# Loads in another order: a smaller first slice, the rotation table last, residual tiles in later steps

## The chip, the cores and the metric

The kernel runs on one core of a Trainium2 chip. A core has a matrix engine (TensorE, PE in the profile; its weight loads are PEld), a vector engine (VectorE, DVE), an engine for functions of one variable (ScalarE, ACT), a general one (GpSimd, POOL) and SyncE (SP), which here only issues transfers (DMAs). Each engine has its own queue of instructions, and semaphores tie the queues together. Sixteen DMA engines carry out the transfers of all queues. The metric is the device time of one execution in microseconds, the median of several.

## The reference

One layer of a streaming encoder, on x of 1024 frames by 1024 channels, all in 32-bit floats:

```
h = rms_norm(x, g_mix);  z = h @ w_in          # queries, keys, values, indexer, gates, ...
y_a = chunked attention with relative bias     # 4 heads, 9 chunks of 64 frames
y_b = attention on the 256 keys that an indexer picks for each frame
      # index score = sum over 4 heads of relu(q_i . k_i) * w_i, q_i and k_i rotated (rope)
y_c = gated linear recurrence over time
merged = sum over the three branches of sigmoid(gate) * (y @ w_branch)
x = x + merged @ w_out
gu = rms_norm(x, g_ffn) @ w_ffn_in;  x = x + (silu(gu[:, :2816]) * gu[:, 2816:]) @ w_ffn_out
```

What matters here are the two ends: the norm of x with the product that gives the indexer's 324 columns (256 query, 64 key, 4 weights), and the last product, with the residual x added to it.

## The kernel before

**Precision.** Every large product runs on operands that are split in two: `hi`, the value rounded to the matrix engine's format (an ACT copy, line 101), and `lo`, what is left (a DVE subtraction, line 102). `mm3` (lines 116 to 119) then issues three matmuls: hi by hi (L117), hi by the right side's lo (L118), lo of the left side by hi (L119). In the profile nearly all matmuls therefore stand on these three lines, and nearly all splits on lines 101 and 102; the names of the tiles tell them apart.

**Buffers.** `Slots` keeps a list of equal buffers in SBUF: `get` takes the one that was freed first, `free` puts one back at the end. A tile in a buffer that was used before waits until the last use of the old one is over. `sl` is the large pool, `ring` a small one (seven buffers at the start, 31 in the last product).

**Order.** A planner of the tile framework arranges the instructions of each engine by its own estimate of when their inputs are ready; the order of the program is kept only where `keep_in_program_order` says so, as for the loads that this case is about. [...]

**The start.** x is read twice: as rows (for the norm's sum of squares, on ACT, line 187) and transposed (as the left side of products). The eight tiles of 128 frames come in batches of 1, 1, 2, 2 and 2 (`BATCH`). The SyncE queue gets the rows and transposes of batch 0, the small constants `sm`, the index weights in slices of k (`W0K`; k runs over eight blocks of 128 channels, 324 columns each), batch 1, batch 2, the rotation table `ctab` (512 KB), batches 3 and 4. For each batch GpSimd computes the reciprocal root, PE spreads it over partitions (L190), DVE scales the transposed tile (L197), ACT and DVE split it (hTh, hTl). `split_w0`, called in the k loop of batch 0, splits a slice of weights (w0h, w0l). PE then runs 24 matmuls of 324 columns for each tile of 128 frames (G<-w0h,hTh and so on). The rotation table is first used by DVE on lines 279 and 280, when four tiles are through.

**The last product.** Activations come from HBM, where the feed-forward step has left them (`pair_dram`, tile fa<-pd), the weights from `w_fo` (fw). It is a Strassen-like scheme: four passes m = 0 to 3 of eleven steps kk each, 44 steps; a step of passes 0 to 2 has 24 matmuls of 512 columns. `prep1` to `prep4` load and split the operands of a step, and `prepare` calls them four steps ahead (`AHEAD`). The eight tiles of the residual x (`load_x`, tile xr<-x2d, 512 KB each) are loaded in pass 0, one in each of `prep1(3)` to `prep1(10)`, behind the loads of that step. Tiles 0 to 3 are first added to (L1329) at the end of pass 0, tiles 4 to 7 (L1346) at the end of pass 1. All these loads share SyncE's queue; GpSimd's queue writes the last results of the feed-forward step at the same time.

Of the kernel before, what the change touches and what calls it, by code (L numbers as in the profile page):

```python
# [10 lines left out]
F32 = mybir.dt.float32  # L11
# [68 lines left out]
def hybrid_kernel(ctx: ExitStack, tc: tile.TileContext, x, xt, small, cs, bias_a, lru_w, w_idx, w_zg, w_c, w_g, w_b,  # L80
                  w_o, w_fi, w_fo, out):
    nc = tc.nc
# [5 lines left out]
    ring = Slots(arena, range(NRING))  # L88
# [7 lines left out]
    def smc(name, j=0, n=1):  # L96
        o, _ = SMALL_OFF[name]
        return sm[:, o + j:o + j + n]

    def split(raw, hi, lo, eng=None):  # L100
        S.activation(hi, raw, AF.Copy)  # L101
        (eng or V).tensor_tensor(lo, raw, hi.bitcast(F32), op=OP.subtract)  # L102
# [21 lines left out]
    def rsqrt(dst, src, n, scale):  # L124
        v = const.tile([128, n], F32, name="rs_v", tag=f"rsv{n}", bufs=2)
        G.tensor_scalar(v, src, scale, EPS, op0=OP.mult, op1=OP.add)
        G.tensor_tensor(dst, v, mhalf[:, 0:n], op=OP.pow)
# [7 lines left out]
    def sbank(shape=(128, 1024)):  # L135
        return psum.tile(list(shape), F32, name="S", tag="S", bufs=2)
# [6 lines left out]
    hT = [(sl.get((128, T), F32R, "hTh"), sl.get((128, T), F32R, "hTl")) for _ in range(KD)]  # L143

    w0 = []
    W0K = ((0, 3), (3, 3), (6, 2))

    def load_w0():
        for k0, kn in W0K:
            raw = ring.get((128, kn, 324), F32, "w0r")  # L150
            tc.keep_in_program_order(nc.sync.dma_start(raw, w_idx[:, k0:k0 + kn, :]))
            w0.append([k0, kn, raw])

    def split_w0(q):
        k0, kn, raw = w0[q]
        hi, lo = ring.get((128, kn, 324), F32R, "w0h"), ring.get((128, kn, 324), F32R, "w0l")
        split(raw, hi, lo)
        ring.free(raw)
        w0[q] = (k0, kn, hi, lo)
# [4 lines left out]
    for t0, tn in BATCH:  # L164
        for t in range(t0, t0 + tn):
            xts[t] = sl.get((128, D), F32, "x")
            tc.keep_in_program_order(nc.sync.dma_start(xts[t], x[t * 128:(t + 1) * 128, :]))
        kn = KD // tn
        ps_ = []
        for n in range(tn):  # L170
            c0 = 1024 * (t0 + n)
            pt = sl.get((128, kn, 128 * tn), F32, "xT")
            tc.keep_in_program_order(nc.sync.dma_start(pt.rearrange("p k t -> p (k t)"), xt[:, c0:c0 + 1024]))
            ps_.append(pt)
        parts.append(ps_)
        if t0 == 0:
            tc.keep_in_program_order(nc.sync.dma_start(sm, small))
            load_w0()
        if t0 == 2:
            ctab = sl.get((128, NT, 2, 64), F32, "cs")  # L180
            tc.keep_in_program_order(nc.sync.dma_start(ctab, cs))
    junk = sl.get((128, D), F32, "junk")
    for (t0, tn), ps_ in zip(BATCH, parts):
        w = 128 * tn
        rb = sbank((128, w))
        for t in range(t0, t0 + tn):
            S.activation(junk, xts[t], AF.Square, accum_out=ss_x[:, t:t + 1])
        rsqrt(rs_x[:, t0:t0 + tn], ss_x[:, t0:t0 + tn], tn, 1.0 / D)
        for t in range(t0, t0 + tn):
            PE.transpose(rb[:, 128 * (t - t0):128 * (t - t0) + 128], rs_x[:, t:t + 1].to_broadcast([128, 128]), ident)  # L190
        kn = KD // tn
        for k in range(KD):
            if t0 == 0 and k in (0, 3, 6):
                split_w0(k // 3)
            r = ps_[k // kn][:, k % kn]
            hi, lo = (a[:, 128 * t0:128 * t0 + w] for a in hT[k])
            V.scalar_tensor_tensor(r, r, smc("g_mix", k), rb, op0=OP.mult, op1=OP.mult)  # L197
            split(r, hi, lo)
        sl.free(*xts[t0:t0 + tn], *ps_)
# [1032 lines left out]
    ring = Slots(arena, fore + rw.free_list + rr.free_list + sl.free_list[:9])  # L1232
# [4 lines left out]
    def load(t, src):  # L1237
        tc.keep_in_program_order(nc.sync.dma_start(t, src))
        return t

    def split_pair(raw, n=2):
        if n == 1:
            t = ring.get((128, 2, 512), F32R, "fo")
            split(raw, t[:, 0:1], t[:, 1:2])
            return t[:, 0:1], t[:, 1:2], t
        hi, lo = ring.get((128, 2, 512), F32R, "foh"), ring.get((128, 2, 512), F32R, "fol")
        split(raw, hi, lo)
        return hi, lo, hi, lo
# [3 lines left out]
    def load_x(t):  # L1252
        xr.append(load(sl.get((128, D), F32, "xr"), x2_dram[t]))

    def split_act(m, kk):
        raw = load(ring.get((128, 2, 512), F32, "fa"), pair_dram[m][kk])
        a = split_pair(raw)
        ring.free(raw)
        return a

    def weights(kk, q):
        return load(ring.get((128, 2, 512), F32, "fw"), w_fo[kk, :, q:q + 2])

    def prep1(kk):
        B = weights(kk, 0)
        a = split_act(0, kk)
        if kk > 2:
            load_x(kk - 3)
        w = split_pair(B)
        ring.free(B)  # L1270
        return a, w

    def prep2(kk):
        B = ring.get((128, 512), F32, "fw")
        load(B, w_fo[kk, :, 1])
        b34[kk] = load(sl.get((128, 2, 512), F32, "fw2"), w_fo[kk, :, 2:4])
        a = split_act(1, kk)
        ts = ring.get((128, 2, 512), F32, "T12")
        V.tensor_sub(ts[:, 0], b34[kk][:, 0], B)
        V.tensor_sub(ts[:, 1], b34[kk][:, 1], ts[:, 0])  # L1280
        w = split_pair(ts)
        ring.free(ts, B)
        return a, w
# [12 lines left out]
    def prep4(kk):  # L1296
# [12 lines left out]

    plan = [  # L1310
        (prep1, ((0, 0, 1), (1, 1, 0))),
        (prep2, ((0, 1, 1), (1, 0, 0))),
        (prep3, ((0, 0, 0), (1, 1, 1))),
        (prep4, ((1, 0, 0),)),
# [158 lines left out]
```

## Time and profile before

| | |
|---|---|
| median of 3 runs | 1534.41 us (1532.22 to 1535.24) |
| the profiled execution | 1535.26 us, its span 1533.5 us |
| mean granted TensorE clock | 0.989 of full |
| PE, PEld busy | 1475.8 us (96%), 1233.4 us (80%) |
| DVE, ACT, POOL busy | 1127.5 us (74%), 760.6 us (50%), 110.6 us (7%) |
| DMA | 182.59 MB, 119 GB/s over the span |

An engine's busy time is the time in which at least one of its instructions ran, so PE can be busy and still wait a little between matmuls; "idle before" is the stretch in which an engine ran nothing, and the arrow behind it names what ended it. The last product runs from about 1320 us to the end. A fence below holds whole lines of a view; "..." stands for lines left out.

### The profile page before, as it was taken

The numbers are of one execution on the slowest core, as the hardware profiler recorded it, in microseconds if no ns is written. First come the engines' busy times: TensorE is split into PE (matmuls) and PEld (weight loads), VectorE is DVE, ScalarE is ACT, GpSimd is POOL, SyncE is SP. The second block draws the span as 40 slices with busy tenths as digits, with TensorE's granted clock in tenths as the row PEclk, the third lists the DMA queues.
The fourth block names the chain that finished last, engine by engine and source line by source line (L and its number), as shares of the span: only waits on it lengthen the run. The fifth ranks groups of instructions, "written<-read, shape, count | busy, mean of one in ns | idle before, by whom it ended". The sixth has DMA issues, their size and how long they took to land.

```text
span 1533.5 us, 19936 instructions
## 1 busy us (share of the span) xinstructions
PE 1475.8 (96%) x7556; PEld 1233.4 (80%) x7556; DVE 1127.5 (74%) x1997; ACT 760.6 (50%) x1204; POOL 110.6 (7%) x161
## 2 busy tenths in 40 slices
PE   6999899999999998999998989999999999999999
PEld 5898688989788976788886868888888888788887
DVE  6889989869666779767889786555555556478973
ACT  6557767865778656443114563333333333354440
POOL 1220011210000200110000200000000000000000
PEclk9999999999999999999999999999999999999999
DMA  7011213112111131358551322323232323697532
GB/s 285 28 46 54 85 32 110 31 68 84 55 54 43 44 106 44 133 170 319 188 196 66 115 91 97 110 96 110 96 110 97 110 96 124 247 349 267 191 125 89
DMA packets 52240, 182.59 MB, mean 119 GB/s; under 512 B 6000, under 2 KB 6128, under 8 KB 52144
## 3 DMA queue, kind: packets, MB, share of 16 engines
q1 hardware_dynamic: 38448, 135.17, 25.6%
q0 software_dynamic: 11968, 43.00, 7.2%
q10 hardware_dynamic: 1728, 3.15, 0.5%
q8 instruction: 59, 0.97, 0.3%
q14 instruction: 37, 0.30, 0.1%
HBM read 135.94 MB, written 45.35 MB: 118 GB/s over the span
## 4 chain that ended last, share of the span: by engine, by line
PE 63%; DVE 6%; issue 2%; ACT 2%; DMA 2%; POOL 0%; SPq 0%; ACTq 0%; POOLq 0%; DVEq 0%
PE B L118 14%; PE B L119 14%; PE B L117 14%; PE G L119 3%; PE G L117 3%; PE G L118 3%; PE T L118 1%; PE T L119 1%; PE T L117 1%; DMA fa<-pd 1%; PE S L117 1%; PE S L118 1%; PE S L119 1%; PE T L426 1%; PE T L418 1%
## 5 line engine op out<-in xcount | busy, mean ns | idle before, releaser
L118 PE MATMUL B<-hl,fwh 128*128 128x512 f32 x528 | 205.4, 391 | 2.8 <-DVE hl L102 2.8
L117 PE MATMUL B<-hh,fwh 128*128 128x512 f32 x528 | 202.7, 391 | 3.3 <-ACT hh L101 3.3
L119 PE MATMUL B<-hh,fwl 128*128 128x512 f32 x528 | 198.4, 391 | 0.0
L117 PEld LDWEIGHTS B<-hh,fwh 128*128 128x128 f32 x528 | 99.5, 188 | 25.0 <-ACT hh L101 4.2
L118 PEld LDWEIGHTS B<-hl,fwh 128*128 128x128 f32 x528 | 99.7, 189 | 24.4 <-DVE hl L102 3.9
L119 PEld LDWEIGHTS B<-hh,fwl 128*128 128x128 f32 x528 | 99.6, 189 | 20.7
L118 PE MATMUL G<-wzl,hTh 128*128 128x256 f32 x384 | 112.1, 293 | 3.5 <-DVE wzl L102 3.5
L117 PE MATMUL G<-wzh,hTh 128*128 128x256 f32 x384 | 110.9, 291 | 3.8 <-ACT wzh L101 3.1
L119 PE MATMUL G<-wzh,hTl 128*128 128x256 f32 x384 | 111.9, 292 | 0.0
L102 DVE TENSOR_TENSOR fwl<-s,fwh 128x1024 fp32r<-128x1024 f32 x44 | 53.9, 1224 | 77.9 <-PE B L118 75.1
L117 PE MATMUL B<-foh,foh 128*128 128x512 f32 x264 | 102.9, 396 | 2.1 <-ACT foh L101 2.1
L118 PE MATMUL B<-fol,foh 128*128 128x512 f32 x264 | 102.7, 389 | 0.0
L119 PE MATMUL B<-foh,fol 128*128 128x512 f32 x264 | 101.7, 389 | 0.0
L655 ACT ACTIVATE junk_s<-score,ngS 128x1024 int8<-128x1024 f32 (+2 forms) x78 | 77.5, 993 | 17.8 <-DVE ngS L653 13.7
L117 PEld LDWEIGHTS G<-wzh,hTh 128*128 128x128 f32 x384 | 75.3, 197 | 5.8 <-ACT wzh L101 3.7
L118 PEld LDWEIGHTS G<-wzl,hTh 128*128 128x128 f32 x384 | 75.4, 196 | 5.1 <-DVE wzl L102 4.1
L119 PE MATMUL G<-hTh,wgl 128*128 128x512 f32 x192 | 75.8, 395 | 2.0 <-DVE wgl L102 2.0
L117 PE MATMUL G<-hTh,wgh 128*128 128x512 f32 x192 | 75.8, 395 | 1.1 <-ACT ge L550 1.1
L119 PEld LDWEIGHTS G<-wzh,hTl 128*128 128x128 f32 x384 | 75.6, 197 | 0.7 <-issue 0.5
L118 PE MATMUL G<-hTl,wgh 128*128 128x512 f32 x192 | 75.5, 393 | 0.0
L101 ACT ACTIVATE fw<-fb 128x512 fp32r<-128x512 f32 x22 | 13.9, 634 | 121.4 <-PE B L119 120.5
L101 ACT ACTIVATE foh<-fa 128x1024 fp32r<-128x1024 f32 x33 | 35.0, 1060 | 58.7 <-DMA fa<-pd 39.5
(486 smaller groups left out, 3859.0 us busy)
## 6 DMA issues: line engine op xcount, KB each, us to landing
fw<-in_w_fo SPq DMA_DIRECT2D x33, 512.0 KB, 5.6
fa<-pd SPq DMA_DIRECT2D x33, 512.0 KB, 5.0
gl<-gd SPq DMA_DIRECT2D x24, 512.0 KB, 5.3
fa<-in_w_fi SPq DMA_DIRECT2D x22, 512.0 KB, 3.5
fb<-in_w_fi SPq DMA_DIRECT2D x22, 512.0 KB, 3.5
pd<-act POOLq DMA_DIRECT2D x22, 512.0 KB, 5.2
ga<-in_w_g SPq DMA_DIRECT2D x18, 512.0 KB, 3.6
x<-in_x SPq DMA_DIRECT2D x16, 512.0 KB, 7.2
```

Of the source, the lines that this page charges most:

```text
L101: S.activation(hi, raw, AF.Copy)
L102: (eng or V).tensor_tensor(lo, raw, hi.bitcast(F32), op=OP.subtract)
L117: PE.matmul(o, lhsT=lh, rhs=rh, start=first, stop=False, **kw)
L118: PE.matmul(o, lhsT=lh, rhs=rl, start=False, stop=False, **kw)
L119: PE.matmul(o, lhsT=ll, rhs=rh, start=False, stop=last, **kw)
L418: PE.transpose(pt[:, b - c0], P[:, 128 * b:128 * b + 128], ident)
L426: PE.matmul(o[64 * e:64 * e + 64, :], lhsT=v[(b0 + b) // 4][:, (b0 + b) % 4, h, :], rhs=PT[e][:, b, :], start=b == 0, stop=b == nb - 1, sk ...
L655: S.activation(junk_s[:, 0:(i + 1) * 128], score[i], AF.Sign, bias=self.ng.bitcast(F32)[:, j:j + 1], accum_out=self.cnt[:, j:j + 1])
```

## The change

Three edits, all to the order or the size of loads:

- The index weights come in slices of 2, 3 and 3 blocks of k, not 3, 3 and 2. The splits follow (k = 0, 2, 5, not 0, 3, 6).
- The rotation table is loaded behind the last batch of x, not behind the third.
- The residual tiles 0 to 3 are loaded in `prep1(6)` to `prep1(9)`, and tiles 4 to 7 in `prep2(1)` to `prep2(4)`, in the second pass.

```diff
-    W0K = ((0, 3), (3, 3), (6, 2))
+    W0K = ((0, 2), (2, 3), (5, 3))
...
-            load_w0()
-        if t0 == 2:
+            for q in range(len(W0K)):
+                load_w0(*W0K[q])
+        if t0 == 6:
             ctab = sl.get((128, NT, 2, 64), F32, "cs")
...
-            if t0 == 0 and k in (0, 3, 6):
-                split_w0(k // 3)
+            if t0 == 0 and k in (0, 2, 5):
+                split_w0((k + 1) // 3)
...
     def prep1(kk):
         B = weights(kk, 0)
         a = split_act(0, kk)
-        if kk > 2:
-            load_x(kk - 3)
+        if 6 <= kk < 10:
+            load_x(kk - 6)
...
     def prep2(kk):
...
         a = split_act(1, kk)
+        if 0 < kk < 5:
+            load_x(kk + 3)
```

`load_w0` now loads one slice of given place and size, and is called once for each.

## Rows read from the trace of the kernel before

**Rows 1.** The page's part 1: busy us, share of the span, instructions of each engine.

```profile
PE 1475.8 (96%) x7556; PEld 1233.4 (80%) x7556; DVE 1127.5 (74%) x1997; ACT 760.6 (50%) x1204; POOL 110.6 (7%) x161
```

**Rows 2.** Timeline of PE, 1337.6 to 1344: start, us, line, operation [idle before].

```profile
1337.78 0.39 PE L119 MATMUL B<-foh,fol 128*128 128x512 f32 x1
1340.28 3.60 PE L117 MATMUL B<-foh,foh 128*128 128x512 f32 x8 [2.11 <-ACT foh L101]
1343.72 0.39 PE L118 MATMUL B<-fol,foh 128*128 128x512 f32 x1
```

**Rows 3.** Windows: length, busy of PE, PEld, DVE, ACT, POOL; clock; DMA share; GB/s.

```profile
1320.00:1340.00 20.00, 18.16 (x81) 14.71 (x79) 8.35 (x10) 7.09 (x7) 2.14 (x4) 1.00 1.00 383
1340.00:1360.00 20.00, 19.72 (x80) 16.21 (x81) 14.88 (x13) 10.72 (x11) 0.00 (x0) 0.91 1.03 409
1360.00:1380.00 20.00, 20.00 (x89) 16.54 (x89) 16.12 (x21) 9.34 (x9) 0.00 (x0) 1.00 0.82 297
```

**Rows 4.** Waits of PE, 0 to 60 us: in total, times, longest.

```profile
PE G L119 <- DVE hTl L102: 2.4, 5, 1.2
PE G L117 <- ACT w0h L101: 2.4, 1, 2.4
```

**Rows 5.** Timeline of SyncE's queue, 1317 to 1330 (issues, not transfers).

```profile
1318.66 0.43 SPq L1238 DMA_DIRECT2D xr<-x2d  x1
1319.27 0.36 SPq L1238 DMA_DIRECT2D fw<-in_w_fo  x1
...
1321.65 0.44 SPq L1238 DMA_DIRECT2D xr<-x2d  x1
...
1322.75 0.48 SPq L1238 DMA_DIRECT2D fa<-pd  x1
...
1327.13 0.32 SPq L1238 DMA_DIRECT2D fa<-pd  x1
```

**Rows 6.** DMA issues of 1319.27, 1321.65, 1322.75, each alone: KB, us to landing.

```profile
fw<-in_w_fo SPq DMA_DIRECT2D x1, 512.0 KB, 9.4
...
xr<-x2d SPq DMA_DIRECT2D x1, 512.0 KB, 13.4
...
fa<-pd SPq DMA_DIRECT2D x1, 512.0 KB, 15.4
```

**Rows 7.** Timeline of ACT, 1323 to 1341.

```profile
1331.30 1.06 ACT L101 ACTIVATE foh<-fa 128x1024 fp32r<-128x1024 f32 x1 [5.45 <-DMA fa<-pd]
1337.02 1.06 ACT L101 ACTIVATE foh<-fw 128x1024 fp32r<-128x1024 f32 x1 [4.66 <-DMA fw<-in_w_fo]
1338.22 1.06 ACT L101 ACTIVATE foh<-fa 128x1024 fp32r<-128x1024 f32 x1
1339.18 1.04 ACT L101 ACTIVATE foh<-fw 128x1024 fp32r<-128x1024 f32 x1
```

**Rows 8.** Timeline of DVE, 1325 to 1345.

```profile
1341.59 1.22 DVE L102 TENSOR_TENSOR fol<-fw,foh 128x1024 fp32r<-128x1024 f32 x1
```

**Rows 9.** Timeline of ACT, 4 to 16.

```profile
8.31 1.01 ACT L101 ACTIVATE w0h<-w0r 128x972 fp32r<-128x972 f32 x1 [0.31 <-DMA w0r<-in_w_idx]
```

**Rows 10.** Timeline of DVE, 6 to 16.

```profile
9.53 1.16 DVE L102 TENSOR_TENSOR w0l<-w0r,w0h 128x972 fp32r<-128x972 f32 x1
```

**Rows 11.** Timeline of SyncE's queue, 0 to 25.

```profile
9.50 0.33 SPq L181 DMA_DIRECT2D cs<-in_cs  x1
```

**Rows 12.** DMA issue of 9.50 alone: KB, us to landing.

```profile
cs<-in_cs SPq DMA_DIRECT2D x1, 512.0 KB, 9.8
```

**Rows 13.** Timeline of DVE, 25 to 35.

```profile
29.07 3.22 DVE L197 SCALAR_TENSOR_TENSOR xT<-xT,sm,S 128x256 f32<-128x256 f32 x8 [3.40 <-PE S L190]
...
33.22 0.68 DVE L279 TENSOR_TENSOR t<-zq,cs 128x512 f32<-128x512 f32 x1
```

**Rows 14.** Window of 186 to 200, columns as in rows 3.

```profile
186.00:200.00 14.00, 7.94 (x45) 7.04 (x47) 13.67 (x44) 8.83 (x19) 0.00 (x0) 0.76 0.00 1
```

More of the change, by code (lines that the diff above doesn't have):

```diff
@@ L145, in hybrid_kernel, with load_w0 @@
     w0 = []
-    W0K = ((0, 3), (3, 3), (6, 2))
[L148 to L152, printed above, removed]
+    W0K = ((0, 2), (2, 3), (5, 3))
+    def load_w0(k0, kn):
+        raw = ring.get((128, kn, 324), F32, "w0r")
+        tc.keep_in_program_order(nc.sync.dma_start(raw, w_idx[:, k0:k0 + kn, :]))
+        w0.append([k0, kn, raw])
     def split_w0(q):
```

## The prediction

> **What bounds the kernel now.** The page's first part comes first: TensorE (PE) is busy 96% of the span [rows 1]. Only a stretch in which PE stands still can therefore give much, and a shift early in the program reaches the end unless a wait that hangs on nothing before it swallows it. So the next view is the waits of PE, stretch by stretch, in the two places that the change touches. In the last product (from 1320 us) PE has one idle stretch worth the name, 2.11 us before 1340.28, ended by a ScalarE (ACT) split, and the eight matmuls behind it take 3.60 us [rows 2]. In the same 20 us the DMA engines are busy all the time, share 1.00 and 383 GB/s, and PE's granted clock, full before, falls to a mean of 0.91 behind the idle time [rows 3]. This is the spot where eight residual tiles (xr) stand among the operand loads. In the first 60 us PE waits 2.4 us for the first slice of index weights, and 2.4 us in five pieces for residuals of the normalised input [rows 4].
>
> **The last product: why PE stands.** The SyncE queue issues, in the order of the program, weights, activation, residual tile, weights, and so on. The first residual tile, xr 0, follows the operands of step 3 (the fourth step), so the queue holds: xr 0 (1318.66), the weights of step 4 (1319.27), its activation, xr 1 (1321.65), the weights of step 5, its activation (1322.75) [rows 5]. The landings are issue plus time to landing [rows 6]: weights of step 4 at 1328.7, xr 1 at 1335.0, activation of step 5 at 1338.2. The splits on ACT start just after landings [rows 7]: activation of step 4 at 1331.30, weights of step 5 at 1337.02, activation of step 5 at 1338.22, and only then, at 1339.18, the weights of step 4, which had been on the chip for 10 us. ACT works off its queue in order, so that split, the last one that step 4 needs, stood behind two splits whose loads were late. At 1340.28 PE starts step 4.
>
> Two tiles (xr 0 and xr 1) stand ahead of the activation of step 5. Without them each load takes the place in the queue of the tile two places before it. The activation of step 5 takes the place of xr 1 and lands at 1335.0, not 1338.2. Its split runs 1335.05 to 1336.1, the weights of step 4 follow to 1337.1. PE is through with step 3 at 1338.00 (the matmul of 1337.78, matmuls being 0.227 us apart at full clock [rows 2]), so it no longer waits for this split. Next in line is the residual of those weights on VectorE (DVE), now 1341.59 to 1342.81 [rows 8], for the first matmul of L118 at 1343.72. On DVE it is fourth of four splits of 1.22 us, and the second of them can start at 1336.1: 1336.1 + 3 x 1.2 = 1339.7. Eight matmuls of L117 from 1338.00 at full clock end at 1339.81. So the L118 matmul would start at 1339.81 where it starts at 1343.72 now: **3.9 us less**, of which 2.3 us are the idle stretch and 1.6 us the eight matmuls at half clock, 1.2 GHz (3.44 us from 1340.28 to 1343.72, against 1.81).
>
> How much a tile ahead is worth is the open size here. With the queue alone it is 512 KB at 409 GB/s [rows 3], 1.28 us; the activation would land at 1338.2 - 2.56 = 1335.6, the DVE chain would end at 1340.3, and PE would lose 0.5 us of the 3.9. Beside GpSimd's four writes of the last feed-forward step a place was worth more: xr 1 landed 3.7 us after the split of the activation of step 4, the load before it, had begun (1335.0 against 1331.30). I take **3.7 us**, bounds 0 and 3.9 (0: the rival below). [...]
>
> Where do the tiles go? xr 0 to 3 follow the loads of steps 6 to 9, issued four steps (4 x 24 x 0.227 = 21.8 us) ahead; their first reader is the add at the end of step 10, at about 1338 + 7 x 5.44 = 1376, some 20 us after the last of them lands. xr 4 to 7 go to steps 12 to 15, are issued at about 1360 to 1380, and are first read by the adds behind step 21, at about 1436. In 1360 to 1380 the DMA share is 0.82 [rows 3]; four tiles add 4 x 1.28 = 5.1 us to some 20 us, so the queue may lag by a microsecond or two, against a lead of 21.8 us. Cost nothing; without that lead it would be at most these 5.1 us.
>
> **The start: the first slice.** It shrinks from 972 to 648 columns, 486 to 324 KB, and lands 166 kB / 400 GB/s = 0.4 us before 8.3; its ACT split takes 0.67 us by columns where it takes 1.01 [rows 9]. PE's first matmul moves forward by 0.4 + 0.3 = 0.7 us. Its second needs the residual on DVE (1.16 us from 9.53 [rows 10], 0.77 by columns), which comes 0.4 us sooner if DVE keeps its order. But the second slice is needed one k sooner (k = 2, not 3; three matmuls, at half clock 0.43 x 324/512 = 0.27 us each, 0.8 us) and the DVE work ahead of it is smaller by 0.4 us only, so 0.4 us can come back as a wait. The slices add up to the same bytes and columns. I take **0.3 us**, bounds -0.5 and 0.7.
>
> **The start: the rotation table.** It leaves its place ahead of x 4, so that x 4 to 7 and their transposes land 1.28 us sooner and the table lands last of the group. Now it is issued at 9.50 [rows 11] and lands 9.8 us later [rows 12], at 19.3; behind eight more tiles it lands at 19.3 + 8 x 1.28 = 29.5. Its first reader starts at 33.22 [rows 13]: 3.7 us of cover, so the move costs nothing; without the cover, the lateness itself. What may be gained: DVE stands 3.40 us before 29.07, waiting for the transposed norm (L190) of tiles 4 and 5 [rows 13], which PE's order has placed for when those tiles were expected. From there DVE runs without a break and PE waits for it, 1.2 us at the longest [rows 4]. If the place moves with the landing, up to 1.28 us. I take **0.7 us**, bounds -0.5 and 1.3. Both parts of the start go through to the end, because PE, busy from there, orders what follows.
>
> **Sum.** 3.7 + 0.3 + 0.7 = 4.7 us. The profiled execution took 1535.26 us (span 1533.5 and 1.76 around it, which nothing touches), so its like would take 1530.6. It was 0.85 us above the median of the runs shown, so the median goes from 1534.41 to **1529.7**.
>
> **Rivals.** (a) The end gives nothing. The order on ACT is not the program's: weights of step 4 behind both splits of step 5 says that a planner placed it by expected times, presumably because its output buffer was still being written out by GpSimd. If it expects that write late, the activation of step 6, now also two places forward, is put ahead of it as well; it takes the landing of 1338.2, its split ends at 1339.28, and the weights of step 4 go at 1339.2 as before. Against it: that load's buffer is that of the activation of step 3, so it is issued only at 1327.13 [rows 5], behind GpSimd's writes. Then only the start is left: 1534.4 - 1.0 = 1533.4, no change. [...]
>
> (b) Slower: the planner orders the middle anew. Between 186 and 200 us DVE is busy 13.67 of 14.00 us and PE 7.94 only, at a mean clock of 0.76 [rows 14]: splits of the next weights wait their turn among other work. That is 6.1 us idle, and at most (1 - 0.76) x 14 = 3.4 us for the clock (half of the 6.7 us at the lower level), 9.4 us in all. If the shifted start makes the planner put one more such split behind the top-k counts in the 100 us where DVE is this full, the price is 9.4 - 4.7 = 4.7 us net, 1539.1. It decides once such waits are worth 4.7 + 3.1 = 7.8 us. For it: nearly every order is the planner's; against it: a shift of all work by a constant leaves the order as it is.
>
> (c) The start turns against the change: PE starts, waits for the second slice, and the table falls late in the order: -0.5 - 0.5 + 3.7 = 2.7 us gained, 1531.7, within what counts as no change.
>
> **Chances.** Forecast 0.53, (a) 0.23, (b) 0.13, (c) 0.11. A difference under 0.2%, 3.1 us, can't be told from none here. Under the forecast the time lies between 1527.5 (start at its upper bounds) and 1531.2. Faster by over 0.2% (below 1531.3): 0.53. Same: (a) and (c), 0.33 with a little of (b): 0.34. Slower (above 1537.5): the rest of (b), 0.13. The range reaches from 1526.0, a new order that happens to save a wait of 1.5 us, to 1536.5, the lower part of (b).
>
> **What would show it.** Right: no idle stretch on PE between 1320 and 1345 and a full clock there; weights of step 4 split by about 1337; xr loads 0 to 3 behind the loads of steps 6 to 9; first matmul at about 8.7 us; less than 3.4 us idle on DVE before tile 4's scaling. Wrong: an ACT split of step 6 ahead of that of step 4, a wait of DVE on the table near 30 us, a PE wait in steps 12 to 15, or new waits on splits between 60 and 900 us.

## The result and the profile after

The changed kernel takes 1525.12 us (median of 4 runs, 1523.58 to 1526.58), the kernel before 1533.46 us beside it (4 runs, 1532.22 to 1535.24). The ratio is 0.9948, 95% interval 0.9936 to 0.996: 6 to 10 us less. The forecast was 1529.7 us, 4.7 us less, and the range began at 1526.0. The sign was right, the size was not.

The profiled execution took 1523.58 us with a span of 1521.8 us. Its first part against that of before [rows 1]:

```profile
PE 1468.5 (96%) x7556; PEld 1227.0 (81%) x7556; DVE 1127.9 (74%) x1997; ACT 760.0 (50%) x1204; POOL 109.3 (7%) x161
```

Nothing was taken out: the counts are those of before, and PE is as busy as it was in share. Of the 11.7 us between the two profiled executions 7.3 are busy time of PE. The same matmuls ran less at half clock: the mean granted clock is 0.995, before 0.989. The rest is idle time.

**The last product.** All of it begins 7.79 us sooner (its forerunner, the last L118 matmul of the feed-forward step, starts at 1312.08, before at 1319.87). The timeline of PE around step 4, against [rows 2], shows no idle time, and the eight matmuls take 1.98 us where they took 3.60:

```profile
1329.98 0.39 PE L119 MATMUL B<-foh,fol 128*128 128x512 f32 x1
1330.21 1.98 PE L117 MATMUL B<-foh,foh 128*128 128x512 f32 x8
1332.03 0.41 PE L118 MATMUL B<-fol,foh 128*128 128x512 f32 x1
```

The windows of the same three stretches as [rows 3], 8 us sooner, have PE at 20.00 of 20.00 us and the clock at 1.00 throughout; the DMA share is as full as before, and fuller in the third stretch (0.92, before 0.82):

```profile
1312.00:1332.00 20.00, 20.00 (x90) 16.44 (x89) 11.51 (x13) 8.35 (x9) 2.14 (x4) 1.00 1.01 379
1332.00:1352.00 20.00, 20.00 (x89) 16.56 (x89) 15.00 (x14) 11.49 (x11) 0.00 (x0) 1.00 1.03 408
1352.00:1372.00 20.00, 20.00 (x90) 16.56 (x89) 16.21 (x22) 6.78 (x7) 0.00 (x0) 1.00 0.92 343
```

SyncE's queue, against [rows 5]: weights and activation of steps 5 and 6 now follow one another, and the first residual tile stands behind them.

```profile
1313.87 0.50 SPq L1238 DMA_DIRECT2D fw<-in_w_fo  x1
1314.42 0.52 SPq L1238 DMA_DIRECT2D fa<-pd  x1
1314.98 0.67 SPq L1238 DMA_DIRECT2D fw<-in_w_fo  x1
1319.90 0.33 SPq L1238 DMA_DIRECT2D fa<-pd  x1
1320.27 0.47 SPq L1238 DMA_DIRECT2D xr<-x2d  x1
```

The activation of step 5 (issue of 1314.42) now lands after 12.8 us, before after 15.4 [rows 6]:

```profile
fa<-pd SPq DMA_DIRECT2D x1, 512.0 KB, 12.8
```

That is 1327.22. Counted from the start of the stage it comes at 15.14 us, before at 18.28: 3.1 us sooner, and where xr 1 landed before (1335.0, 15.1 us after the start of the stage). ACT's rows, against [rows 7], have the order weights of step 5, activations of steps 4 and 5, weights of step 4; DVE, against [rows 8], has those weights' residual done at 1331.88, just ahead of the L118 matmul of 1332.03:

```profile
1323.82 1.06 ACT L101 ACTIVATE foh<-fw 128x1024 fp32r<-128x1024 f32 x1 [5.21 <-DMA fw<-in_w_fo]
1324.79 1.04 ACT L101 ACTIVATE foh<-fa 128x1024 fp32r<-128x1024 f32 x1
1327.29 1.06 ACT L101 ACTIVATE foh<-fa 128x1024 fp32r<-128x1024 f32 x1 [1.46 <-DMA fa<-pd]
1328.26 1.04 ACT L101 ACTIVATE foh<-fw 128x1024 fp32r<-128x1024 f32 x1
...
1330.66 1.22 DVE L102 TENSOR_TENSOR fol<-fw,foh 128x1024 fp32r<-128x1024 f32 x1
```

**The start.** The split of the first slice is ready sooner (timeline of ACT, against [rows 9]), PE's first matmul starts at 8.76, before at 9.38, and DVE stands 3.15 us ahead of the scaling of tiles 4 and 5, before 3.40 [rows 13]:

```profile
7.77 0.74 ACT L101 ACTIVATE w0h<-w0r 128x648 fp32r<-128x648 f32 x1 [2.23 <-DMA w0r<-in_w_idx]
...
8.76 0.64 PE L117 MATMUL G<-w0h,hTh 128*128 128x324 f32 x1 [1.77 <-ACT hTh L101]
...
28.69 3.22 DVE L197 SCALAR_TENSOR_TENSOR xT<-xT,sm,S 128x256 f32<-128x256 f32 x8 [3.15 <-PE S L190]
```

The waits of PE in the first 60 us, against [rows 4]: the wait for the first slice of weights is gone, and others have taken its place.

```profile
PE G L119 <- DVE hTl L102: 3.4, 4, 1.2
PE G L118 <- DVE wzl L102: 2.2, 1, 2.2
PE G L117 <- ACT hTh L101: 1.8, 1, 1.8
```

Up to the first transposition of the tile zA (T<-ident,zA), which ends this part of the program, PE is idle for 16.6 us, before for 16.0: what the first wait gave went into the others. That mark comes at 92.80 us, before at 94.27; up to there this trace has no half clock and that of before 3.4 us.

**The middle.** The prediction had no term between 60 and 1320 us. But where PE turns to the gates of the recurrence (L532, about 385 us) before has three waits of 1.42, 0.45 and 1.08 us:

```profile
386.48 0.50 PE L532 MATMUL S<-us,lwh 128*128 128x512 f32 x1 [1.42 <-DVE us L213]
...
388.15 0.47 PE L532 MATMUL S<-us,lwh 128*128 128x512 f32 x1 [0.45 <-DVE us L213]
...
390.49 0.50 PE L117 MATMUL G<-hTh,wgh 128*128 128x512 f32 x1 [1.08 <-ACT ge L550]
```

and after has two of 0.70 and 0.69 us:

```profile
382.38 0.50 PE L532 MATMUL S<-us,lwh 128*128 128x512 f32 x1 [0.70 <-DVE us L213]
...
385.59 0.33 PE L418 MATMUL T<-ident,P 128*128 128x128 f32 x1 [0.69 <-DVE P L412]
```

No load of the first two edits lies within 300 us of this place, and the third comes 900 us later. What differs is the order that the planner gave the instructions of PE, DVE and ACT from about 340 to 410 us, and once more from about 835 to 875 us; elsewhere between 70 and 1300 us the order is that of before.

### The profile page after: what moved, and what is told of

Its sections match the earlier page's. It is cut to its first block, busy times and chain, and to the rows that moved or that the text cites. A ratio compares the mean times of both kernels' runs of the same rounds, so it can differ in the third digit from the quotient of the medians.

```text
span 1521.8 us, 19934 instructions
## 1 busy us (share of the span) xinstructions
PE 1468.5 (96%) x7556; PEld 1227.0 (81%) x7556; DVE 1127.9 (74%) x1997; ACT 760.0 (50%) x1204; POOL 109.3 (7%) x161
## 3 DMA queue, kind: packets, MB, share of 16 engines
q1 hardware_dynamic: 38448, 135.17, 25.8%
q10 hardware_dynamic: 1728, 3.15, 0.5%
## 4 chain that ended last, share of the span: by engine, by line
PE 76%; DVE 17%; ACT 4%; issue 2%; DMA 1%; ACTq 0%; DVEq 0%; SPq 0%
PE B L119 15%; PE B L118 15%; PE B L117 14%; PE G L119 7%; PE G L118 7%; PE G L117 7%; DVE key L643 3%; PE T L426 2%; PE T L118 1%; PE T L119 1%; PE T L117 1%; PE T L418 1%; PE S L242 1%; PE S L117 1%; DVE ol L102 1%
## 5 line engine op out<-in xcount | busy, mean ns | idle before, releaser
L118 PE MATMUL B<-hl,fwh 128*128 128x512 f32 x528 | 205.1, 391 | 3.6 <-DVE hl L102 3.6
L118 PEld LDWEIGHTS B<-hl,fwh 128*128 128x128 f32 x528 | 99.6, 189 | 24.9 <-DVE hl L102 4.3
L118 PE MATMUL G<-wzl,hTh 128*128 128x256 f32 x384 | 110.8, 289 | 5.8 <-DVE wzl L102 5.7
L118 PE MATMUL B<-fol,foh 128*128 128x512 f32 x264 | 102.7, 389 | 0.0
L655 ACT ACTIVATE junk_s<-score,ngS 128x1024 int8<-128x1024 f32 (+2 forms) x78 | 77.5, 993 | 17.7 <-DVE ngS L653 13.6
L118 PEld LDWEIGHTS G<-wzl,hTh 128*128 128x128 f32 x384 | 73.9, 192 | 7.7 <-DVE wzl L102 6.7
L118 PE MATMUL G<-hTl,wgh 128*128 128x512 f32 x192 | 75.6, 394 | 0.0
L1182 DVE TENSOR_TENSOR act<-act,B 128x512 f32<-128x512 f32 x22 | 15.1, 687 | 65.5 <-PE B L119 65.5
```

The source lines that it names most:

```text
L118: PE.matmul(o, lhsT=lh, rhs=rl, start=False, stop=False, **kw)
L655: S.activation(junk_s[:, 0:(i + 1) * 128], score[i], AF.Sign, bias=self.ng.bitcast(F32)[:, j:j + 1], accum_out=self.cnt[:, j:j + 1])
L1182: V.tensor_add(a1, a1, x)
```

## The experiments

Two explanations stood against each other. Theory 1: the end gives what was forecast, the start about 1 us, and the rest is the planner's new order in the middle, which neither of the first two edits triggers alone. Theory 2: what lies beyond the end comes from the start's own loads, or from chance in the clock. All ratios are against the kernel before in the same series, 1533.4, 1533.1 and 1532.7 us. 0.1% is 1.5 us.

### The whole change, its halves, and the first edit alone

The changed kernel once more, without an edit.

> The changed kernel once more, in five rounds. Theory 1 (the start edits gave some 4.5 us, through a new order of the planner in the middle as well, the residual tiles 3.9): 8 us under the kernel before again, ratio 0.9945 to 0.9955. Theory 2 (the start gave 1.5 us, the residual tiles 3.9, and the rest was that the granted clock happened to fall less often in the runs that were compared): 5 to 6 us, ratio 0.996 to 0.9968.

Measured: 1525.87 us (5 runs), ratio 0.9951 [0.9939, 0.9964], as theory 1 had it; the interval reaches just into theory 2's range.

The third edit alone:

```diff
-        if kk > 2:
-            load_x(kk - 3)
+        if 6 <= kk < 10:
+            load_x(kk - 6)
...
+        if 0 < kk < 5:
+            load_x(kk + 3)
```

> The third edit alone: residual tiles 0 to 3 in prep1(6) to prep1(9), tiles 4 to 7 in prep2(1) to prep2(4); the start as before. Both theories: PE does not stand at the start of step 4 of the last product, the clock stays up there, 3.9 us less than before (ratio 0.9975). Up to 1320 us every engine has the order of before, so the time to there should agree with before within the scatter of the clock, some 2 us.

Measured: 1527.11 us (5 runs), 0.9962 [0.9948, 0.9975]: 3.8 to 8.0 us less, so the expected 3.9 lies at the edge of the interval. The trace has no wait of PE in the last product, and that stage is 3.9 us shorter (table of stages below).

The first two edits, the residual tiles as before:

```diff
-    W0K = ((0, 3), (3, 3), (6, 2))
+    W0K = ((0, 2), (2, 3), (5, 3))
...
-        if t0 == 2:
+        if t0 == 6:
             ctab = sl.get((128, NT, 2, 64), F32, "cs")
```

> The first two edits alone (slices of 2, 3, 3; table behind the last batch), the last product as before. Theory 1: 4 to 5 us less than before (ratio 0.997 to 0.9974): about 1.5 us by 100 us and the rest in the stretches of 360 to 480 and 800 to 860 us, where the order of the engines changes too. Theory 2: 1.5 us (0.999). The 2.1 us of PE before step 4 stay in both.

Measured: 1529.22 us (9 runs), 0.9976 [0.9967, 0.9986]: 3.7 us less, where the prediction had 1.0. Theory 1 had this, theory 2 (1.5 us) did not.

The first edit alone (only the slices of `W0K`):

> The first edit alone: slices of 2, 3 and 3 blocks; table and residual tiles as before. First matmul at 8.7 us, not 9.4. Theory 1 and 2: 0.3 to 0.8 us less at 60 us; beyond 60 us the order of all engines is that of before, so nothing is added there (ratio 0.9993 to 1). If the slice alone gave the whole 1.5 us of the start, the time at 60 us is 1.5 us less.

Measured: 1535.36 us (11 runs), 1.0015 [1.0005, 1.0024]: slower, by 0.8 to 3.7 us. No theory had that sign. Its waits of PE in the first 60 us:

```profile
PE G L117 <- ACT hTh L101: 3.1, 2, 1.9
PE S L242 <- ACT kih L297: 2.8, 1, 2.8
PE G L119 <- DVE hTl L102: 2.7, 2, 2.1
```

The score matmuls (L242) wait 2.8 us for the keys, a wait that neither before nor the whole change has. Ahead of it two waits for the split input are longer, 1.18 us at 31.17 and 2.15 us at 34.39 (before: 0.50 us at 31.17 and 1.23 us at 36.85), and around them the clock falls. From 30 to 50 us its mean is 0.83, where before it was 1.00; before has 0.84 in the next 10 us. Up to the first transposition of zA that makes 6.8 us of half clock, before 3.4 us:

```profile
31.17 0.42 PE L117 MATMUL G<-w0h,hTh 128*128 128x324 f32 x1 [1.18 <-ACT hTh L101]
...
34.39 0.64 PE L119 MATMUL G<-w0h,hTl 128*128 128x324 f32 x1 [2.15 <-DVE hTl L102]
...
30.00:50.00 20.00, 16.68 (x95) 16.24 (x96) 17.66 (x46) 9.70 (x33) 2.09 (x4) 0.83 0.01 2
```

A second trace of the same kernel was taken to see whether that was chance:

> The first slice alone once more, for a second trace. Open is why it was 0.05 to 0.24% slower alone. Reading 1 (its start really is worse: the second slice is late for k = 2, and the clock falls for it): before 94 us there is again more half clock than the 3.4 us of the kernels with the start as before, and 94 us is reached at 94.6 to 95.5, not at 93.8 to 94.3. Reading 2 (chance in where the clock falls): the start is within 0.3 us of before, and the low stretches lie elsewhere.

Measured (one execution, 1539.12 us, beside one of before at 1535.05): the same wait, and the same low clock from 30 to 50 us.

```profile
PE S L242 <- ACT kih L297: 3.4, 1, 3.4
...
30.00:50.00 20.00, 16.71 (x93) 16.28 (x94) 17.39 (x46) 9.42 (x33) 2.09 (x4) 0.83 0.00 2
```

The first transposition of zA comes at 95.11 and 97.78 us in these two traces, at 93.28 to 94.33 in the five with the start as before. Reading 1 holds for the start being worse and for the clock: 6.8 and 10.2 us of half clock up to there, 3.4 in each of the five. The second mark lies beyond its range. The reason that it gave, the late second slice, is not shown: PE waits 0.3 us for that slice's residual at 12.3 us, in the whole change too.

### Is it the start or the order in the middle?

The table alone behind all of x (`t0 == 6`); the order changes in the first 70 us only.

> The rotation table alone moves behind the last batch of x; the order of PE, DVE and ACT differs from before in the first 60 us only. Theory 1 (most of what the first two edits give together comes from a new order of the instructions between 350 and 860 us, which neither makes alone): the stages from 360 us on take as long as before, the start gives 0 to 1 us, ratio 0.9993 to 1.0005. Theory 2 (the gain is in the start itself, from x landing sooner): most of the 3.8 us is here, ratio 0.9975 to 0.9985.

Measured: 1532.26 us (11 runs), 0.9987 [0.9975, 0.9999]. Between the two expectations; the interval reaches into both, so by time this run decides nothing. Its trace does for the middle: the first two waits there are those of before (1.43 and 0.46 us), and so is the length of that stage, 25.83 us. It reaches the first transposition of zB (the first mark of the table of stages below) at 358.46, 1.6 us before the mean of the kernels with the start as before. That can be the clock alone: up to there it has 10.2 us of half clock, each of the five 13.7, and 3.4 us of half clock cost, as an estimate, up to half of that, 1.7 (the eight matmuls of step 4 took 3.44 us at half clock, 1.82 at full).

The table one place later only:

```diff
-        if t0 == 2:
+        if t0 == 4:
             ctab = sl.get((128, NT, 2, 64), F32, "cs")
```

> The slices as before; the table behind batch 3 of x, one place later only. The start is ordered otherwise than in any kernel so far, but from 350 to 400 and from 800 to 860 us PE, DVE and ACT have the order of the changed kernel. Theory 1: those stages are as short as in the changed kernel (360 to 386 us by 1.7 us shorter, 386 to 482 by 0.8, 795 to 858 by 0.5 to 1.5 with the clock), 3 us in all, with 1 us either way for the start: ratio 0.9974 to 0.9987. Theory 2: half of the table's move, under 1 us: 0.9993 to 1.0003.

Measured: 1530.86 us (11 runs), 0.9988 [0.9979, 0.9997]. The middle is as theory 1 said (table below, 24.13 and 95.31 us); the time, 1.8 us less, lies just outside its range, and the interval reaches into that of theory 2, so the stages decide.

Slices of 3, 2 and 3 blocks, the table last: the loads of the change but for one block in the first slice.

```diff
-    W0K = ((0, 3), (3, 3), (6, 2))
+    W0K = ((0, 3), (3, 2), (5, 3))
...
-        if t0 == 2:
+        if t0 == 6:
```

> Slices of 3, 2 and 3 blocks, the table behind all of x: the loads of the changed kernel but for one block of the first slice. The order from 350 to 860 us is that of before; in the last product, about 1380 us, a few splits change places. Theory 1: no gain in the middle, 0 to 1 us from the start, ratio 0.9993 to 1.0005. Theory 2: nearly the gain of both edits of the start, ratio 0.9975 to 0.9985.

Measured: 1531.97 us (11 runs), 0.9993 [0.998, 1.0006]. Theory 1 held: nearly the same loads, the middle's order as before, and the gain of the two edits (0.9976) is not there, though the interval reaches into the upper part of theory 2's range.

The table moved the wrong way, ahead of batch 1 of x:

```diff
-        if t0 == 2:
+        if t0 == 0:
             ctab = sl.get((128, NT, 2, 64), F32, "cs")
```

> The rotation table goes the other way: right behind the index weights, ahead of batch 1 of x, so that all later tiles of x land 1.28 us later. From 350 to 400 and from 800 to 860 us the order of PE, DVE and ACT is nonetheless that of the changed kernel. Theory 1 (the gain beyond the start is that order): the waits of PE between 360 and 400 us fall from 3.0 to 0.9 us in all, the stages from 360 to 930 us take 3 to 4 us less, the start loses 0 to 1.5 us; ratio 0.9975 to 0.9995. Theory 2 (the gain comes from x landing sooner): slower, ratio 1.0002 to 1.001.

Measured: 1530.57 us (11 runs), 0.9987 [0.9978, 0.9995]: faster, by 0.8 to 3.4 us, although seven tiles of x land later. Theory 2 falls here. PE's waits in the middle are those of the new order:

```profile
385.25 0.47 PE L532 MATMUL S<-us,lwh 128*128 128x512 f32 x1 [0.15 <-DVE us L213]
387.10 0.33 PE L418 MATMUL T<-ident,P 128*128 128x128 f32 x1 [0.70 <-DVE P L412]
```

Why this order is better is seen on DVE. Before, other work stands ahead of the two splits of the recurrence's input (us) and between them; the second starts 1.57 us after the first:

```profile
383.61 1.37 DVE L229 TENSOR_TENSOR kl<-T,kh 64x512 fp32r<-64x512 f32 x2
385.02 0.16 DVE L411 RECIPROCAL rc<-sum 128x1 f32<-128x1 f32 x1
385.21 1.22 DVE L213 TENSOR_TENSOR us<-u,us 64x1024 fp32r<-64x1024 f32 x1
386.46 0.29 DVE L412 TENSOR_SCALAR P<-P,rc 128x128 f32<-128x128 f32 x1
386.78 1.22 DVE L213 TENSOR_TENSOR us<-u,us 64x1024 fp32r<-64x1024 f32 x1
```

In the kernel with the first two edits they follow each other, ahead of the division and of the two key splits (kl) that come between in the rows above:

```profile
382.05 2.47 DVE L213 TENSOR_TENSOR us<-u,us 64x1024 fp32r<-64x1024 f32 x2
384.55 0.16 DVE L411 RECIPROCAL rc<-sum 128x1 f32<-128x1 f32 x1
384.75 1.40 DVE L229 TENSOR_TENSOR kl<-T,kh 64x512 fp32r<-64x512 f32 x2
```

So the first of them ends at about 383.3, just when PE is through with its product (383.32); before it ended at 386.43, 1.4 us after PE was.

### How many tiles may stand ahead of the activation of step 5?

In these three the start is as before and only `load_x` moves. Two tiles out of the way, the others behind the loads of steps 7 to 10 and in the second pass:

```diff
-        if kk > 2:
-            load_x(kk - 3)
+        if kk > 4:
+            load_x(kk - 5)
...
+        if 0 < kk < 3:
+            load_x(kk + 5)
```

> The start as before; of the third edit only this: residual tiles 0 to 5 behind the loads of steps 5 to 10, tiles 6 and 7 in the second pass. So only two tiles leave the place ahead of the activation of step 5. Theory 1 (two places in the queue before one landing are what the end gives): the idle stretch of 2.1 us before step 4 and the eight matmuls at half clock are gone, 3.9 us less after 1320 us, ratio 0.9962 to 0.9978, as with the whole third edit. Rival (the transfers compete, so all eight tiles count): an idle stretch of 0.5 to 1.5 us stays between 1335 and 1360, 1.5 to 3 us less, ratio 0.998 to 0.999.

Measured: 1529.63 us (7 runs), 0.9974 [0.9963, 0.9985], 2.3 to 5.7 us less. PE's rows have no idle time, as with the whole edit:

```profile
1336.30 1.98 PE L117 MATMUL B<-foh,foh 128*128 128x512 f32 x8
```

One tile out of the way:

```diff
-        if kk > 2:
-            load_x(kk - 3)
+        if kk > 3:
+            load_x(kk - 4)
...
+        if kk == 1:
+            load_x(7)
```

> The start as before; residual tiles 0 to 6 one step later than before, tile 7 in the second pass: one tile, not two, stays ahead of the activation of step 5. Theory 1 (each place in the queue delays that landing by 1.3 to 3.3 us): a wait of PE between 0 and 1.5 us stays before step 4, 1.3 to 3.9 us less after 1320 us, ratio 0.9975 to 0.9995. Rival (the splits' order on ACT decides, and one tile doesn't change it): wait and half clock as before, 0.9995 to 1.0005.

Measured: 1529.94 us (12 runs), 0.9987 [0.9976, 0.9999]. Two short waits of PE stay, and the clock does not fall (1.00 from 1335 to 1355 us):

```profile
1334.00 2.12 PE L117 MATMUL B<-foh,foh 128*128 128x512 f32 x8 [0.91 <-ACT foh L101]
1336.59 0.50 PE L118 MATMUL B<-fol,foh 128*128 128x512 f32 x1 [0.47 <-DVE fol L102]
```

Two tiles more in the way:

```diff
-        if kk > 2:
-            load_x(kk - 3)
+        if 0 < kk < 9:
+            load_x(kk - 1)
```

> The start as before; residual tiles 0 to 7 behind the loads of steps 1 to 8, two steps sooner than before: four tiles, not two, stand ahead of the activation of step 5, and two ahead of that of step 3. Theory 1: that landing is two places later, so the wait of PE in steps 2 to 5 grows from 2.1 us to between 4.5 and 8 us, and the stretch after 1320 us by 2 to 7 us: ratio 1.0013 to 1.0045. Rival (GpSimd's writes at that time set the landings, not the places in the queue): the stretch stays within 1 us of before, 0.9995 to 1.0007.

Measured: 1534.17 us (11 runs), 1.0016 [1.0007, 1.0025], slower as theory 1 said and the rival did not. The wait is 3.4 us, less than the 4.5 to 8 expected, because the two places more delayed the landing by 1.4 us in all (below), not by 1.3 to 3.3 each:

```profile
1337.57 3.78 PE L117 MATMUL B<-foh,foh 128*128 128x512 f32 x8 [3.41 <-ACT foh L101]
```

### All traces side by side

Lengths of stages in us, from the starts of the matmuls that bound them: to the first T<-ident,zB; from there to the first S<-us,lwh; to the last G<-hTl,wcyh; and from the last L118 of the feed-forward step to the last matmul of the kernel.

| kernel | start to zB | to S<-us | to wcyh | last product |
|---|---|---|---|---|
| before | 360.67 | 25.81 | 96.11 | 209.51 |
| third edit alone | 359.68 | 25.82 | 96.12 | 205.59 |
| two tiles out | 360.15 | 25.82 | 96.14 | 205.59 |
| one tile out | 359.32 | 25.82 | 96.14 | 207.57 |
| four tiles ahead | 360.51 | 25.83 | 96.14 | 212.00 |
| slices alone (two traces) | 360.99, 364.74 | 25.80, 25.82 | 96.17, 98.10 | 208.13, 209.42 |
| table alone | 358.46 | 25.83 | 98.12 | 208.73 |
| slices 3, 2, 3 | 359.96 | 25.83 | 97.71 | 209.53 |
| table at t0 = 4 | 359.79 | 24.13 | 95.31 | 209.31 |
| table at t0 = 0 | 359.72 | 24.19 | 95.33 | 209.57 |
| first two edits | 359.17 | 24.16 | 95.29 | 209.83 |
| the whole change (two traces) | 357.31, 359.07 | 25.07, 24.14 | 95.38, 95.34 | 205.62, 205.59 |

The second and third columns fall into two groups by the order in the middle alone, whatever the loads: 25.8 + 96.1 us with that of before, 24.2 + 95.3 with the new one, **2.5 us** less. The profiled execution of the whole change is the exception, with 25.07: PE came to this stage 1.8 us sooner than in the second trace and waited 0.70 us for a split of us, where the second did not wait; there the order gave 1.5 us. (Three traces with 97.7 to 98.1 have 3.4 to 6.8 us of half clock in that stage, the others none.)

The order from 835 to 875 us changes along with it but saves nothing that shows: from wcyh to the last product, the stretch that the table leaves out, it is 833.4 to 837.3 us in the nine traces with the order of before (mean 835.7), 834.3 to 835.9 in the five with the new one (mean 835.4).

The last column goes by the tiles ahead: 205.6 with none, 207.6 with one, 208.1 to 209.8 with two (mean of eight traces 209.25), 212.0 with four. The landing of the activation of step 5, counted from the start of that stage, goes with it: 14.2 to 15.2 us with none ahead (four traces), 17.1 with one, 17.7 to 18.5 with two (eight, mean 18.2), 19.6 with four.

The first column is noisier: 359.3 to 360.7 with the start as before (five traces, mean 360.07), 357.3 to 359.2 with both edits (three, mean 358.52). The lowest of the three has 6.8 us of half clock in that stage, the five have 13.7 each; without it the mean is 359.12.

## Why the prediction was wrong

**The end: right.** Forecast 3.7 us, measured 3.9 in the profiled pair (209.51 - 205.62) and 3.65 against the mean of the eight traces with two tiles ahead. Each step came as written: the landing sooner by 3.1 us (forecast 3.2), the split of the weights of step 4 directly behind that of the activation of step 5, DVE's chain done 0.15 us ahead of need (forecast 0.1), full clock. By bytes alone, 3.9 - 0.5 = 3.4, it would have been too low: at 409 GB/s two tiles are 2.6 us, the landing moved by 3.1; no run here isolates where the other 0.5 us come from. No trace gives the clock in GHz: the 1.2 of the prediction is what its rows come to, eight matmuls of 512 columns in 3.44 us, 1.19 columns per ns; measured are 0.43 us for each of these eight before, where the granted clock was at half, and 0.23 after.

**Rival (a): fell.** No split of step 6 went ahead of that of the weights of step 4. On ACT the latter starts right behind the split of the activation of step 5 in both traces, 0.96 us after it before (1338.22, 1339.18) and 0.97 us after it now (1327.29, 1328.26). Rival (c) expected a loss at the start; the whole change shows none.

**The moved tiles: right.** No wait of PE appears from 1320 us to the end in the three kernels that move two or more tiles back; four tiles in later steps cost nothing.

**The start, first slice: wrong by itself.** Forecast 0.3 us gained, bounds -0.5 to 0.7; alone it costs 0.8 to 3.7 us. The step that failed is "I take 0.3 us": it followed PE to the third matmul, but the smaller slice changes the order of the whole first 70 us, and there the split input and the keys come late (waits of 2.15 and 2.8 us) and the clock falls (0.83 from 30 to 50 us). Together with the table's move the wait for the keys and that fall of the clock do not arise (1.00 from 30 to 50 us), so in the whole change it did no harm that shows.

**The start, rotation table: right in sign, size not settled.** Forecast 0.7, bounds to 1.3; by time the table alone gave 0.2 to 3.8 us, and the 1.6 us that its trace is ahead at 360 us can be the clock. Both together are 1.55 us ahead there (forecast 1.0), 1.0 without the trace with the least half clock, within the scatter of the traces. The cover was there, as forecast: the table landed at 30.3 (forecast 29.5), and DVE first read it at 37.97 without a wait. DVE's wait that was to shrink by up to 1.28 us shrank by 0.25 only: PE came to L190 at 28.27, before at 28.65, straight from the matmuls ahead of it, so its place in PE's order held it.

**The step that failed: rival (b) and its counterweight.** The prediction set the middle at nothing because "a shift of all work by a constant leaves the order as it is". It does not: the order from 340 to 410 us changed with the two edits of the start, as it did with two other placements of the table, one of them in the opposite direction. Rival (b) had the mechanism, with the price taken from one place where DVE was full and with the sign fixed as a loss; a new order was allowed a gain of 1.5 us at the far end of the range only. It brought 2.5. That is the term that the sum lacked.

**The sum.** 3.7 to 3.9 (end) + 2.5 (order in the middle) + 1.0 to 1.6 (start) = 7.2 to 8.0 us, the last term an estimate within the scatter. Measured: 8.0 us [6.1, 9.8] and 7.5 us [5.5, 9.4]. The two profiled executions differ by more, 11.7 us: that of before was 1.8 us above its median and that of after 1.5 us below, with mean clocks of 0.989 and 0.995. One number of the prediction does not follow from its terms: with the start at its upper bounds the time is 1534.41 - 3.7 - 0.7 - 1.3 = 1528.7, not 1527.5. The forecast and the range do not hang on it.

**Open.** Why the planner changes the order for just these placements was not found: the two edits do it only together, the table alone does it at t0 = 0 and 4 but not at 6. How large the start's part is can't be told from the scatter: 1.0 to 1.6 us at the mark of 360 us, and only 0.5 us at the first transposition of zA (92.80, 93.83 and 93.67 us with both edits, mean 93.92 with the start as before).

## What to carry to other kernels

- Where a planner arranges the instructions, an edit that moves a load has two effects: its own, which can be worked out from the queue, and possibly a new order elsewhere, which the trace of before did not foretell here. It gained 2.5 us in one place; nothing said beforehand that it would not cost as much. Allow for it on both sides of the range, and look for it by setting the two instruction lists side by side before explaining a difference.
- To separate them, make a variant that triggers the same new order with a load change that should hurt, and one with nearly the same loads and the old order.
- A prefetch that is needed late belongs behind the operands that are needed soon; the price of the places ahead of them can be read from the queue and the landings. Here it held to 0.2 us for the two places that were taken away, and was too high for two places more.

## What the runs showed of the hardware

- **Each further place in the queue cost less here**: 2.0 us of the last stage for the first tile, 1.7 for the second, 2.75 for the third and fourth together (differences of the last column, 209.25 for two tiles, with the half clock that followed in most of those traces). The landing itself moved by 2.3, 1.1 and 1.4 us.
- **The clock scatters between executions of one kernel.** Of 78 executions of the kernel before, those at a mean granted clock of 0.988 took 1534.65 us on average (18), those at 0.990 1532.43 (24), those at 0.992 1531.36 (7). A difference of 2 us between two traces can be this alone.
- **The same waits were followed by half clock in one execution and not in another.** Where PE turns to the gates, before waits 1.42 and 0.45 us and has no half clock up to the last G<-hTl,wcyh. The trace of the table alone waits 1.43 and 0.46 us, the second one of the slices alone 1.43 and 0.47, and in both 6.8 us of half clock begin there (at 385.7 and 392.1). The third wait of before, 1.08 us, is then gone: PE idles 0.6 us in that stage in these two, 1.5 us in before.
